# A hybrid block on one core: one of three large products goes back to eight projections, laid between the heads of linear attention, and three engines get a written order there

## The chip, the cores and the metric

The kernel runs on one core of a Trainium2 chip. A core has a matrix engine (PE, with a separate record for its weight loads, PEld), a vector engine (DVE), a scalar engine (ACT), a general engine (POOL) and a queue engine (SP) that here only starts transfers. Each executes its own list of instructions in order, and they wait for each other through semaphores. The metric is the device time of one execution in microseconds; smaller is better.

## The reference

One layer on 512 tokens of width 1024, in fp32. A normalised input is multiplied by w_in into eleven parts; two branches follow, each with a gate from the same projection, and then a feed-forward layer with a squared ReLU.

```
proj = rmsnorm(h, g_mix) @ w_in
(gq, gk, gv, gr, z_gf, z_gb, cq, ckv, kr, z_ma, z_mb) = split(proj)
y_gla = rmsnorm(o_forward + o_backward, g_gla) * silu(gr)      # linear attention, 4 heads, 256 values each
y_mla = softmax attention, 8 heads, q from rmsnorm(cq) @ w_uq, k and v from rmsnorm(ckv) @ w_ukv
merged = sigmoid(z_ma) * y_gla + sigmoid(z_mb) * y_mla
h = h + merged @ w_out;  h = h + relu(rmsnorm(h) @ w_ff1)^2 @ w_ff2;  out = rmsnorm(h, g_final)
```

The linear attention keeps a decay per key feature and token, from a log-sigmoid of a small gate (z_gf forward, z_gb backward). In the kernel z_ma is za and z_mb is zb, each 1024 features wide. The sigmoid is taken as half of 1 + tanh of half the argument.

## The kernel before

Every fp32 product is made of three passes of rounded halves (mm3, lines 88 to 90): high by high, high by low, low by high. Each operand is therefore split once: ACT copies the high half (L93) and DVE subtracts to get the low half (L94); with a scale the two are L97 and L98. Wherever a new weight is used, both engines have to pass it before PE can.

**Projections by features** (proj_begin, proj_run, proj_T). A block of 128 columns of w_in, 512 KB, is loaded on SP's queue into one of three staging buffers, split into one of four pairs of buffers, and multiplied with the eight parts of the transposed input xT: 24 matmuls of 128 features by 512 tokens. The result has features in the rows. The scale of each token, R, is multiplied in afterwards. gq and gk of each head, the eight zb blocks, ckv (two) and cq (three) are made so.

**Products of seven** (class Seven). gr, za and gv, each 1024 wide, are made with tokens in the rows by a 2 x 2 block scheme with seven block products in place of eight, in the order 1, 2, 5, 6, 3, 7, 4. Each product is 24 matmuls of 128 by 512. prepare(m) takes differences of the loaded blocks on DVE (less, L575) and splits them, two products ahead; product(m) runs the matmuls, and its ends copy (ACT, L622) or add (DVE, L627) the partial sums. A sink takes each finished piece: gr_rows (tanh, times), za_rows (tanh with half the row factor, and a multiplication into g1, which holds the gated gr), gv_rows (the split v). Between some products stands a filler: a projection that gives the other engines time (zb4, zb5, z_chunk, gq1, gk1).

**Heads of linear attention.** For each of four heads: gate_parts makes the gates (two matmuls, abs on ACT, min on DVE, exp and log, with a table load before the log and one behind it), then decays (four scans for each direction, a difference, two exps, small factors v3 and e3 on POOL and ACT). gla_qk multiplies q and k with them (four on DVE, L455, and eight products on POOL, L463). gla_scores makes the backward scores bd of four diagonal blocks, which ACT copies out (bds, L498), and then for each of four key blocks three matmuls into sc, a predicated copy of bds on DVE (L512), and a split of sc. bd and sc share four PSUM banks ("at"). gla_out multiplies the scores with v (48 matmuls), squares the result on ACT, multiplies it into g1 on DVE, and POOL makes the factor of each row. gla_turn, which comes after the scores of the next head, scales g1 by this factor, transposes it on PE (eight transposes, L688) and applies the gain on ACT.

**What sets the order.** The program is traced in Python and a planner then orders each engine's instructions by priority, costs and readiness, with tile buffers of fixed number (29 "u2", 26 "u4", four banks each of "mm" and "at"). The programmer can bind instructions of one engine to the traced order (in_program_order) or one group behind another (goes_behind). Before the change PE is bound from the products of seven to the gla_out of head 2; POOL is bound up to the end of the products; ACT and DVE are left to the planner in the heads. Gates of head h + 1 are traced ahead of the scores of head h. The last head mixes with the latent projections (ckv, cq), the rotary tables of head 1 and the first parts of softmax attention.

Of the kernel before, what the change touches and what calls it, by code (L numbers as in the profile page):

```python
# [18 lines left out]
P = 128  # L19
S = 512  # L20
NT = S // P
# [35 lines left out]
def tile_block(ctx: ExitStack, tc: tile.TileContext, t, out: bass.AP):  # L57
# [346 lines left out]
    def gate_parts(h, tag="at"):  # L404
        l = u4("l", F32)
        ms = []
        for i, d in enumerate(("f", "b")):
            bcol = (V_BF if d == "f" else V_BB) + h
            bias = gvec[:, bcol : bcol + 1]
            acc = ps(tag, f"gate{d}")  # L410
# [6 lines left out]
        nc.scalar.activation(l, l, AF.Ln, bias=1.0)  # L417
        return {d: decays(d, l[:, i], ms[i]) for i, d in enumerate(("f", "b"))}
# [220 lines left out]
    def za_rows(i, half, src, dst):  # L639
        nc.scalar.activation(dst, src, AF.Tanh, scale=r_half[:, i : i + 1])  # L640
        g = g1[i, half]
        nc.vector.scalar_tensor_tensor(g, dst, 1.0, g, op0=ALU.add, op1=ALU.mult)

# [4 lines left out]
    def mla_g2(f):  # L648

        return gated(proj_T(C_ZB + f * P, f"zb{f}"), f"b{f}")[1]  # L650

    out_rs = {}

    def gla_out(h, sc):
# [3 lines left out]
        c = slice(at, at + GDV)  # L658
        for i in range(NT):
            o = accs[i // 2][:, (i % 2) * GDV : (i % 2 + 1) * GDV]  # L660
            tok = slice(i * P, (i + 1) * P)
            for j in range(NT):
                mm3(o, sc[j][:, 0, tok], sc[j][:, 1, tok], v[j, half][:, 0, c], v[j, half][:, 1, c],
                    j == 0, j == NT - 1)
        tot = sm(f"gla{h}ss")
        for i in range(NT):
            o = accs[i // 2][:, (i % 2) * GDV : (i % 2 + 1) * GDV]
            junk = u2(f"gla{h}sq")
            nc.scalar.activation(junk[:, 0:GDV], o, AF.Square, accum_out=tot[:, i : i + 1])
            g = g1[i, half][:, c]  # L670
            nc.vector.tensor_tensor(g, o, g, op=ALU.mult)
# [3 lines left out]
        out_rs[h] = tot  # L675

    def gla_turn(h, early=None):

        half, at = h // 2, (h % 2) * GDV
        for i in range(NT):  # L680
            g = g1[i, half][:, at : at + GDV]
            nc.vector.tensor_scalar(g, g, out_rs[h][:, i : i + 1], None, op0=ALU.mult)
        began = traced()
        for dv in range(2):
# [6 lines left out]
            y = u2(f"y1{f}")  # L691
            nc.scalar.activation(y, tp, AF.Copy, scale=gla_gain[:, f : f + 1])
# [5 lines left out]
    def latent(col, n, gcol, name):  # L698
        cs, sqs = [], []
        for j in range(n):  # L700
            if j == 0:
                begun = proj_begin(w_in, col, f"{name}0")
                acc = proj_run(begun, xT)
                yield
            else:
                acc = proj_T(col + j * P, f"{name}{j}")
            c = u2(f"{name}c{j}")
            nc.scalar.activation(c, acc, AF.Copy, scale=gvec[:, gcol + j : gcol + j + 1])
            s = u2(f"{name}s{j}")
            nc.scalar.activation(s, acc, AF.Square)  # L710
            if sqs:
                nc.vector.tensor_tensor(s, s, sqs[-1], op=ALU.add)
            cs.append(c)
            sqs.append(s)
        yield
        diag = feature_rstd(sqs[-1], n * P, name, True)
        yield
        rs = spread(diag, name, "mm")
        res = []
        for j in range(n):  # L720
            nc.vector.tensor_tensor(cs[j], cs[j], rs, op=ALU.mult)
            hl = u4(f"{name}hl{j}")
            split(hl[:, 0, :], hl[:, 1, :], cs[j])
            res.append(hl)
        yield res
# [190 lines left out]
    steps = [(a, m) for a in range(3) for m in SEVEN]  # L916
# [3 lines left out]
    for n, (a, m) in enumerate(steps):  # L920
        ahead = steps[n + 2] if n + 2 < len(steps) else None
        filled = (a, m) in fillers
        if a + 1 < 3:
            for x in {3: (0,), 7: (2, 1), 4: (3,)}.get(m, ()):
                sevens[a + 1].load(x)
# [5 lines left out]
        if ahead:  # L931
            sevens[ahead[0]].prepare(ahead[1])
            if n == 2:
                more_x_sums()
        if (a, m) == (1, 5):
# [3 lines left out]
        if (a, m) == (1, 4):  # L939
            split_gates()  # L940
        if not filled:
            sevens[a].product(m)
        if a == 2 and m == 5:
            parts = gate_parts(0, "mm")
    in_program_order(summed, (mybir.EngineType.Pool,))
    near, nxt, far = gla_qk(0, parts)
    for h in range(GH):
        last = h == GH - 1
        if not last:
            parts = gate_parts(h + 1, "mm")  # L950
        began = traced()
        if last:
            next(ckv_steps)
            marks = [traced()]
            next(cq_steps)
            marks.append(traced())
            next(ckv_steps)
            marks.append(traced())
            next(cq_steps)
            goes_behind((marks[1], marks[2]), (marks[0], marks[1]), PE_ONLY)  # L960
            goes_behind((marks[2], traced()), (marks[1], marks[2]), PE_ONLY)
            ckv = next(ckv_steps)
            next(cq_steps)
            zb = proj_T(C_ZB + 6 * P, "zb6")
        projected = traced()
# [403 lines left out]
```

## Time and profile before

| | us |
|---|---|
| median of three runs | 805.8 |
| lowest, highest | 804.67, 806.24 |
| the profiled execution | 805.88 |
| its span | 803.9 |
| PE busy in the span | 766.5 |
| DVE, ACT, POOL busy | 595.8, 451.6, 103.9 |

The span runs from the first to the last instruction of the program; the profiled execution's own time is 2.0 us more. Times in rows of the profile are from the start of the span. A matmul's end is modelled and covers part of the next one, so the pace of PE is read from starts, not from the 0.39 us that one matmul of 512 columns is given. In a row of groups the columns are: how many, busy time and mean duration in ns, and the idle time of that engine before them with what ended it. In rows of stretches each engine has its busy time and number of instructions, followed by the granted clock of PE, the share of the transfer engines and their rate.

### The profile page before, as it was taken

The numbers are of one execution on the slowest core, as the hardware profiler recorded it, in microseconds if no ns is written. First come the engines' busy times: TensorE is split into PE (matmuls) and PEld (weight loads), VectorE is DVE, ScalarE is ACT, GpSimd is POOL, SyncE is SP. The second block draws the span as 40 slices with busy tenths as digits, with TensorE's granted clock in tenths as the row PEclk, the third lists the DMA queues.
The fourth block names the chain that finished last, engine by engine and source line by source line (L and its number), as shares of the span: only waits on it lengthen the run. The fifth ranks groups of instructions, "written<-read, shape, count | busy, mean of one in ns | idle before, by whom it ended". The sixth has DMA issues, their size and how long they took to land.

```text
span 803.9 us, 10168 instructions
## 1 busy us (share of the span) xinstructions
PE 766.5 (95%) x3744; PEld 645.5 (80%) x3744; DVE 595.8 (74%) x886; ACT 451.6 (56%) x761; POOL 103.9 (13%) x182
## 2 busy tenths in 40 slices
PE   9999999977868699999999999999999999999996
PEld 7778888866757688888898898888888888888885
DVE  7699787977667535889994378784878576857695
ACT  8556555665365434598882256643663366345644
POOL 0400000023523410332120100000000000000014
PEclk9999999988989799999999999999999999999999
DMA  9626243004111021323104462156014611460002
GB/s 333 204 78 187 63 114 117 0 5 124 30 27 31 23 29 50 78 62 98 53 27 163 140 221 59 48 157 183 27 53 147 177 44 53 132 183 26 27 1 104
DMA packets 87041, 73.94 MB, mean 92 GB/s; under 512 B 15088, under 2 KB 66288, under 8 KB 86992
## 3 DMA queue, kind: packets, MB, share of 16 engines
q1 hardware_dynamic: 85904, 70.14, 29.3%
q10 hardware_dynamic: 864, 2.38, 0.8%
q0 software_dynamic: 224, 0.79, 0.3%
q8 instruction: 29, 0.48, 0.3%
q14 instruction: 20, 0.16, 0.1%
HBM read 69.62 MB, written 2.10 MB: 89 GB/s over the span
## 4 chain that ended last, share of the span: by engine, by line
PE 80%; DVE 8%; ACT 5%; issue 2%; DMA 2%; POOL 2%; SPq 1%; POOLq 0%; ACTq 0%; DVEq 0%
PE f L89 7%; PE f L90 7%; PE f L88 7%; PE gx L88 4%; PE gx L89 4%; PE gx L90 4%; PE wo L90 2%; PE wo L89 2%; PE gz L89 2%; PE gz L90 2%; PE gz L88 2%; PE wo L88 2%; PE tp L877 1%; DMA grw<-in_w_in 1%; DVE gvw L575 1%
## 5 line engine op out<-in xcount | busy, mean ns | idle before, releaser
L1133 DVE TENSOR_TENSOR w<-w,w 128x1024 f32<-128x1024 f32 x32 | 38.7, 1221 | 0.4
L1308 POOL DMA_DIRECT2D gfin<-in_g_final x1 | 0.7, 653 | 282.7 <-PE f L90 282.7
L506 PE MATMUL sc<-qkf 128*128 128x128 f32 x32 | 7.9, 335 | 17.5 <-ACT bds L498 17.5
L863 ACT ACTIVATE e<-s,top 128x512 f32<-128x512 f32 x32 | 22.1, 694 | 2.6 <-DVE top L860 2.4
L1080 DVE TENSOR_TENSOR h<-gx,h 128x512 f32<-128x512 f32 x32 | 21.6, 685 | 1.8 <-PE gx L90 1.8
L94 DVE TENSOR_TENSOR pT<-tp,pT 128x512 fp32r<-128x512 f32 x32 | 21.7, 680 | 1.0 <-ACT pT L93 0.7
L506 PEld LDWEIGHTS sc<-qkf 128*128 128x128 f32 x32 | 6.7, 232 | 19.3 <-ACT bds L498 18.7
L860 DVE TENSOR_REDUCE top<-s 128x1 f32<-128x512 f32 x32 | 21.8, 681 | 0.1
L93 ACT ACTIVATE pT<-tp 128x512 fp32r<-128x512 f32 x32 | 19.2, 600 | 3.4 <-PE tp L877 3.3
L877 PE MATMUL tp<-ident,e 128*128 128x128 f32 x128 | 19.3, 273 | 0.2
L88 PE MATMUL av<-pT,v 128*128 128x256 f32 x64 | 19.1, 298 | 0.0
L1186 ACT ACTIVATE fa<-f 128x512 f32<-128x512 f32 x32 | 18.5, 578 | 0.0
L877 PEld LDWEIGHTS tp<-ident,e 128*128 128x128 f32 x128 | 15.2, 140 | 4.1 <-ACT e L863 0.7
L89 PE MATMUL av<-pT,v 128*128 128x256 f32 x64 | 18.4, 287 | 0.0
L90 PE MATMUL av<-pT,v 128*128 128x256 f32 x64 | 18.2, 284 | 0.0
L93 ACT ACTIVATE gbh<-y 128x512 fp32r<-128x512 f32 x16 | 10.2, 635 | 14.0 <-DVE y L1203 14.0
L895 POOL TENSOR_TENSOR tb<-tb,y 128x512 f32<-128x512 f32 x8 | 11.2, 1400 | 50.3 <-DVE tb L894 36.0
L93 ACT ACTIVATE b_20h<-w 128x1024 fp32r<-128x1024 f32 x7 | 7.4, 1059 | 12.1 <-PE gz L90 6.0
L93 ACT ACTIVATE b_10h<-w 128x1024 fp32r<-128x1024 f32 x7 | 7.4, 1059 | 12.1 <-PE gz L90 6.0
L93 ACT ACTIVATE b_00h<-w 128x1024 fp32r<-128x1024 f32 x7 | 7.4, 1057 | 12.0 <-PE gz L90 6.0
L88 PE MATMUL s<-kbuf,q 96*128 96x512 f32 x32 | 13.9, 436 | 0.2 <-DVE pT L94 0.2
L1195 ACT ACTIVATE px<-fa 128x256 f32<-128x256 f32 x32 | 13.4, 419 | 1.0
(1638 smaller groups left out, 2912.9 us busy)
## 6 DMA issues: line engine op xcount, KB each, us to landing
w<-in_w_ff SPq DMA_DIRECT2D x64, 256.0 KB, 3.6
grw<-in_w_in SPq DMA_DIRECT2D x8, 512.0 KB, 7.8
zaw<-in_w_in SPq DMA_DIRECT2D x8, 512.0 KB, 4.2
gvw<-in_w_in SPq DMA_DIRECT2D x8, 512.0 KB, 4.9
x<-in_xt SPq DMA_DIRECT2D x8, 256.0 KB, 5.1
vw<-in_w_first SPq DMA_DIRECT2D x8, 256.0 KB, 5.2
h<-in_x ACTq DMA_DIRECT2D x4, 512.0 KB, 5.1
out<-ms SPq DMA_DIRECT2D x7, 256.0 KB, 2.2
```

The lines of the kernel that those rows point to most:

```text
L88: nc.tensor.matmul(acc, lh, rh, start=start, stop=False, skip_group_check=onto)
L89: nc.tensor.matmul(acc, lh, rl, start=False, stop=False, skip_group_check=onto)
L90: nc.tensor.matmul(acc, ll, rh, start=False, stop=stop, skip_group_check=onto)
L93: nc.scalar.activation(hi, src, AF.Copy)
L94: rest.tensor_tensor(lo, src, raw(hi), op=ALU.subtract)
L506: nc.tensor.matmul(sc[:, dj], near["f"][:, 1, j], near["f"][:, 0, j], start=True, stop=True)
L860: nc.vector.tensor_reduce(top, acc, axis=AX.X, op=ALU.max, negate=True)
L863: nc.scalar.activation(e, acc, AF.Exp, bias=top, accum_out=tot)
L877: nc.tensor.transpose(tp[:, k * P : (k + 1) * P], e[:, k * P : (k + 1) * P], ident)
L1080: nc.vector.tensor_tensor(hc, acc, hc, op=ALU.add)
L1133: nc.vector.tensor_tensor(wq[dst][g], wq[x][g], wq[y][g], op=op)
L1186: nc.scalar.activation(a, acc, AF.Relu)
```

## The change

za is no longer a product of seven. It becomes eight projections by features, za0 to za7, two for each head of linear attention. za_gate multiplies the result by R, takes the tanh and turns it into gain x (1 + tanh) with one ACT operation; gla_turn multiplies this with the transposed output on DVE, in place of the gain on ACT. gla_out is split in three: the matmuls (gla_out), the squares and the row factor (gla_squares), and one DVE operation that applies row factor and gate together (gla_gated) in place of two.

gate_parts is split into gates_begin (up to the log) and gates_end (the decays). The generator for the latent projections becomes a class with the same steps. In the seven scheme gv now follows gr; z_chunk moves to gr's product 7, gq1 to gv's product 2, and the loads and splits of the gates move with them. gv's last two products, gk1 and zb5 are written out ahead of the heads.

In the heads the scores come first, then the next head's gates. From the first gate to the turn of head 2, ACT and DVE (SPLITTERS) are bound to the traced order and PE's bound order is extended to the same point. The rotary tables are traced after this stretch. The turn of each of the first three heads now comes at the end of its own head.

```diff
+    def za_gate(f, acc):
+
+        z = u2(f"za{f}")
+        nc.vector.tensor_tensor(z, acc, R, op=ALU.mult)
+        nc.scalar.activation(z, z, AF.Tanh, scale=0.5)
+        gain = gla_gain[:, f : f + 1]
+        nc.scalar.activation(z, z, AF.Identity, bias=gain, scale=gain)
+        za_gates[f] = z
...
+    def gla_gated(h, os, rs):
+
+        half, at = h // 2, (h % 2) * GDV
+        for i, o in enumerate(os):
+            g = g1[i, half][:, at : at + GDV]
+            nc.vector.scalar_tensor_tensor(g, o, rs[:, i : i + 1], g, op0=ALU.mult, op1=ALU.mult)
...
-            y = u2(f"y1{f}")
-            nc.scalar.activation(y, tp, AF.Copy, scale=gla_gain[:, f : f + 1])
+            y = za_gates.pop(f)
+            nc.vector.tensor_tensor(y, tp, y, op=ALU.mult)
...
-    sevens = [Seven(C_GR, "gr", gr_rows), Seven(C_ZA, "za", za_rows), Seven(C_GV, "gv", gv_rows)]
+    sevens = [Seven(C_GR, "gr", gr_rows), Seven(C_GV, "gv", gv_rows)]
...
-        (0, 2): lambda: zb_gate(4), (0, 7): lambda: zb_gate(5), (1, 2): lambda: z_chunk("mm"),
-        (1, 7): lambda: project_qk(1, 0), (2, 7): lambda: project_qk(1, 1),
+        (0, 2): lambda: zb_gate(4), (0, 7): lambda: z_chunk("mm"),
+        (1, 2): lambda: project_qk(1, 0),
...
+    heads_from = traced()
+    gated_now = gates_begin(0)
+    w_k = begin_qk(1, 1)
+    parts = gates_end(gated_now)
+    sevens[1].product(7)
     near, nxt, far = gla_qk(0, parts)
+    w_b = begin(C_ZB + 5 * P, "zb5")
+    qk[1, 1] = qk_normed(1, 1, proj_run(w_k, xT))
+    sevens[1].product(4)
+    w_a = begin_za(0)
+    g2.append(gated(proj_run(w_b, xT), "b5")[1])
+    ckv_, cq_ = Latent(C_CKV, 2, V_KV, "ckv"), Latent(C_CQ, 3, V_Q, "cq")
+    for h in range(GH - 1):
         sc = gla_scores(near, nxt, far)
+        gated_now = gates_begin(h + 1)
+        w_b = begin_za(2 * h + 1)
+        acc = proj_run(w_a, xT)
+        parts = gates_end(gated_now)
+        za_gate(2 * h, acc)
+        os = gla_out(h, sc)
+        near, nxt, far = gla_qk(h + 1, parts)
+        if h < 2:
+            w_a = begin_qk(h + 2, 0)
         else:
+            ckv_.begin(0)
+        rs = gla_squares(h, os)
+        za_gate(2 * h + 1, proj_run(w_b, xT))
+        if h < 2:
+            w_b = begin_qk(h + 2, 1)
+            gla_gated(h, os, rs)
+            qk[h + 2, 0] = qk_normed(h + 2, 0, proj_run(w_a, xT))
+            w_a = begin_za(2 * h + 2)
+            qk[h + 2, 1] = qk_normed(h + 2, 1, proj_run(w_b, xT))
+        else:
+            ckv_.run(0)
+            ckv_.begin(1)
+            gla_gated(h, os, rs)
+            ckv_.run(1)
+            cq_.begin(0)
+        gla_turn(h)
+    in_program_order(heads_from, SPLITTERS)
+    in_program_order(ordered, PE_ONLY)
...
+    h = GH - 1
+    cos, sin = rotary_tables()
...
+    sc = gla_scores(near, nxt, far)
...
+    za_gate(6, proj_T(C_ZA + 6 * P, "za6"))
...
+    za_gate(7, proj_T(C_ZA + 7 * P, "za7"))
```

More of the change, by code (lines that the diff above doesn't have):

```diff
@@ L919, in tile_block @@
         sevens[a].prepare(m)
-    for n, (a, m) in enumerate(steps):
-        ahead = steps[n + 2] if n + 2 < len(steps) else None
+    for n, (a, m) in enumerate(steps[:-2]):
+        ahead = steps[n + 2]
         filled = (a, m) in fillers
-        if a + 1 < 3:
+        if a == 0:
             for x in {3: (0,), 7: (2, 1), 4: (3,)}.get(m, ()):
-                sevens[a + 1].load(x)
+                sevens[1].load(x)
         if filled:
@@ L930, in tile_block @@
             goes_behind((at, traced()), loading, (mybir.EngineType.SP,))
[L931 to L935, printed above, removed]
+        sevens[ahead[0]].prepare(ahead[1])
+        if n == 2:
+            more_x_sums()
+        if (a, m) == (0, 5):
             load_gates()
@@ L1000, in tile_block @@
+    kbuf = rotary_k()
+    zb = proj_begin(w_in, C_ZB + 7 * P, "zb7")
+    at = traced()
+    proj_run(zb, xT, None, range(3))
+    mid = traced()
+    ro = rotary_q()
+    goes_behind((mid, traced()), (at, mid), PE_ONLY)
+    g2.append(gated(proj_run(zb, xT, None, range(3, KD)), "b7")[1])
+    for _ in up_units(0):
+        pass
+    os = gla_out(h, sc)
+    rs = gla_squares(h, os)
+    gla_gated(h, os, rs)
     LAG_B, LAG_C = 3, 6
```

169 lines of the change are left out of this document (70 added, 99 removed).

## The prediction

> **What bounds the kernel now.** I read the page first (span, granted clock), then the table of busy time by stretches with its edges laid on the stages, then the waits, and last the timeline of one head, engine by engine.
>
> ```profile
> span 803.9 us, 10168 instructions
> ...
> PEclk9999999988989799999999999999999999999999
> ...
> 40.60:92.15 51.55, 49.60 (x218) 40.39 (x216) 47.11 (x56) 29.02 (x38) 1.94 (x4) 1.00 0.42 128
> 92.15:139.30 47.15, 47.15 (x210) 39.04 (x209) 39.46 (x45) 26.37 (x35) 0.00 (x0) 1.00 0.33 98
> 139.30:167.10 27.80, 27.80 (x123) 22.71 (x121) 26.59 (x35) 20.47 (x26) 3.35 (x6) 1.00 0.00 0
> 167.10:195.30 28.20, 19.71 (x75) 15.72 (x74) 18.95 (x23) 16.18 (x22) 5.02 (x15) 0.86 0.28 75
> 195.30:224.00 28.70, 26.16 (x130) 22.85 (x131) 19.73 (x36) 11.23 (x24) 16.18 (x33) 0.84 0.14 37
> 224.00:255.40 31.40, 24.50 (x139) 21.71 (x138) 23.59 (x42) 18.49 (x33) 10.80 (x26) 0.89 0.13 34
> 255.40:288.35 32.95, 24.67 (x137) 21.80 (x136) 18.50 (x39) 18.06 (x33) 11.26 (x27) 0.84 0.12 23
> 288.35:340.20 51.85, 51.85 (x287) 44.74 (x286) 33.14 (x61) 24.87 (x49) 9.98 (x12) 1.00 0.26 50
> ```
>
> Columns: stretch, its length, then busy time and count for PE, PEld, DVE, ACT, POOL, then the clock. The stretches are gr (40.6), za (92.15), gv (139.3), the end of gv (167.1), heads 0, 1 and 2 of linear attention, and the last head up to attention. PE is full everywhere except in the four rows from 167.1 to 288.35. There it sits idle for 8.5, 2.5, 6.9 and 8.3 us, and the clock column is below 1. Nothing else in front of PE is worth moving; the question is what those four rows hold.
>
> ```profile
> PE sc L506 <- ACT bds L498: 17.5, 3, 8.3
> ...
> 224.51 0.67 ACT L412 ACTIVATE l<-gatef,gvec 128x512 f32<-128x512 f32 x1
> 225.08 0.68 ACT L412 ACTIVATE l<-gateb,gvec 128x512 f32<-128x512 f32 x1
> 225.79 1.06 ACT L416 ACTIVATE l<-l 128x1024 f32<-128x1024 f32 x1
> 226.87 1.28 ACT L417 ACT_TABLE_LOAD   x1
> 228.16 1.06 ACT L417 ACTIVATE l<-l 128x1024 f32<-128x1024 f32 x1
> 229.23 1.28 ACT L441 ACT_TABLE_LOAD   x1
> ...
> 233.98 0.58 ACT L498 ACTIVATE bds<-bd 128x512 f32<-128x512 f32 x1
> 234.46 0.62 ACT L434 ACTIVATE eeb<-difb 128x512 f32<-128x512 f32 x1
> ...
> 224.03 1.05 PE L494 MATMUL bd<-qkb 128*128 128x128 f32 x8
> 224.92 0.39 PE L506 MATMUL sc<-qkf 128*128 128x128 f32 x2
> ...
> 225.80 0.39 PE L506 MATMUL sc<-qkf 128*128 128x128 f32 x2
> ...
> 234.62 0.80 PE L506 MATMUL sc<-qkf 128*128 128x128 f32 x2 [6.90 <-ACT bds L498]
> ...
> 243.73 0.28 PE L88 MATMUL gla1o<-gv,sc 128*128 128x256 f32 x1
> ...
> 249.49 0.40 PE L88 MATMUL gk<-xT,gk3h 128*128 128x512 f32 x1
> ```
>
> The waits and head 1 tell why. The scores write bd and four sc tiles into four banks, so the fourth sc needs bd's bank, which the 0.58 us copy bds frees. That copy stands on ACT behind the gates of the next head (abs, exp, two table loads, log): bd is done by 225, bds runs at 233.98. PE waits 6.90 us for half a microsecond of work.
>
> **What PE needs and what it loses.** In the za row PE is never idle: seven products of 24 matmuls, one more projection of 24 (gq1) and z_chunk's 16 make 208 in 47.15 us, 0.2267 each, so 24 cost 5.44 and a pair of gates 0.45. From the starts above: bd 0.89, a score block 0.88, so scores 4.41; gla_out 249.49 - 243.73 = 5.76; the eight transposes of a turn, like bd's eight, 0.89. The four low rows hold 9 x 24 matmuls (gv7, gk1, gv4, gq2, gk2, gq3, gk3, ckv0, ckv1), three scores, three gla_out, three gate pairs, two turns: 49.0 + 13.2 + 17.3 + 1.35 + 1.8 = 82.6 us of work in 121.25. **38.6 us** are lost there, 26 idle and the rest to half clock. That is all the change can win back.
>
> **PE work of the change.** za loses 7 x 24 matmuls and gains 8 x 24: **+5.44**. All other products are the same and only move (zb5, gk1, gv7 and gv4 into the fixed sequence, z_chunk into gr, gq1 into gv, the third turn ahead of the last head, za6 and za7 into the last head).
>
> **What it loses afterwards** needs the new order laid out by hand with these rows.
>
> ```profile
> L93 ACT ACTIVATE sc<-sc 128x512 fp32r<-128x512 f32 x12 | 6.5, 595 | 0.0
> L93 ACT ACTIVATE ckv0h<-ckv0f 128x1024 fp32r<-128x1024 f32 x1 | 1.1, 1063 | 4.9 <-PE gq L89 4.9
> L708 ACT ACTIVATE ckvc<-ckv,gvec 128x512 f32<-128x512 f32 x1 | 0.7, 682 | 0.0
> ...
> L94 DVE TENSOR_TENSOR sc<-sc,sc 128x512 fp32r<-128x512 f32 x12 | 7.6, 685 | 3.0 <-ACT sc L93 3.0
> L426 DVE TENSOR_TENSOR_SCAN rrf<-mf,l 128x128 f32<-128x128 f32 x12 | 5.3, 500 | 3.4 <-ACT l L417 3.4
> L426 DVE TENSOR_TENSOR_SCAN rrb<-mb,l 128x128 f32<-128x128 f32 x12 | 4.3, 402 | 0.0
> L455 DVE TENSOR_TENSOR qkb<-gkn,eeb 128x512 f32<-128x512 f32 x3 | 3.3, 1100 | 0.0
> L512 DVE COPY_PREDICATED sc<-after,bds 128x128 f32<-128x128 int32 x12 | 3.0, 296 | 5.5 <-ACT bds L498 4.1 <-PE sc L508 1.4
> L455 DVE TENSOR_TENSOR qkb<-gqn,eeb 128x512 f32<-128x512 f32 x3 | 2.0, 682 | 0.0
> L94 DVE TENSOR_TENSOR ckv0l<-ckv0f,ckv0h 128x1024 fp32r<-128x1024 f32 x1 | 1.7, 1664 | 0.2 <-ACT ckv0h L93 0.2
> L94 DVE TENSOR_TENSOR ckv1l<-ckv1f,ckv1h 128x1024 fp32r<-128x1024 f32 x1 | 1.2, 1226 | 0.2 <-ACT ckv1h L93 0.2
> ```
>
> Neighbours on an engine overlap by about 0.1 us (225.08 starts before 224.51 + 0.67), so I lay them 0.1 closer than they last; a scan steps 0.32.
>
> Head h, time 0 at bd. The scores now stand ahead of the gates on ACT, so bds ends at 1.7 (behind the last multiplication of the turn before, at 1.1) and the fourth sc, at 3.5, waits for nothing: **the 17.5 us are gone**. What is late next? In the fixed order DVE and ACT hand each score tile to and fro (predicated copy, high half, low half: 1.6), the next beginning after: 8.4 for four. ACT is free at 7.75: two abs 9.1, exp 10.15, table 11.45, log 12.5, high half of za's second weights 13.55; DVE its low half 14.8, four scans and a difference 16.75, again for the other direction 18.7; ACT two exps and e3 20.15, tanh and Identity of the first za gate (priced like sc's copies) 21.4, high half of gq's weights 22.45. DVE meanwhile z (19.4) and the four products of gla_qk (22.8; two at 0.68, two at 1.1 beside POOL), then gq's low half, 1.23 alone or 1.66 beside POOL: 24.1 to 24.5. PE reaches gq at 4.41 + 0.45 + 5.44 + 5.76 + 5.44 = 21.5, runs the two matmuls that need no low half, and waits: 24.3 - 21.95 = **2.4 us**, in each of heads 0, 1 and 2 (ckv0 there). The first za projection and gla_out (sc ready at 8.4, wanted at 10.3) and the second za (14.8, wanted at 16.1) wait for nothing, gk's low half (28.7) is ahead of PE's 29.7. The gating by row factor is now one DVE operation for two, with POOL's factor due by 33 and some 4 us early.
>
> Head 2 has two more: ckv1's split begins only after ckv0's two copies: 0.68 + 0.6 + 1.06 + 1.23 less overlaps and the two early matmuls = **3.0**; cq0's the same behind ckv1, less the turn's 0.89: **2.2**.
>
> Before head 0 (zero at the end of gv's product 3): gates first, ACT two sinks, abs, exp, table, log, gk1's high half 7.5, low half 8.8; PE, done with product 7 at 5.9, waits 2.4. Product 4 adds onto the banks that DVE must first have read for product 7, and these reads stand behind all scans: scans and differences from 8.8 to 12.8, first read 13.5, ACT's high half of v behind the last exp 14.9, DVE's low half 15.6 (each near 0.7, like sc's), second read 16.3. PE wants that bank at 8.8 + 22 x 0.2267 + 0.7 = 14.5: 1.8. Then gla_qk ends at 21.1 and zb5's low half, behind it, at 22.4; PE has finished product 4 at 21.1 and two matmuls at 21.5: 0.9. Together 5.1, with rounding **5.2**.
>
> So the waits are 5.2 + 3 x 2.4 + 3.0 + 2.2 = 17.6.
>
> **Clock.** What a gap costs beside itself:
>
> ```profile
> 54.38 0.50 PE L90 MATMUL zb<-xT,zb4l 128*128 128x512 f32 x1 [1.63 <-DVE zb4l L94]
> ...
> 204.35 0.79 PE L506 MATMUL sc<-qkf 128*128 128x128 f32 x2 [2.29 <-ACT bds L498]
> ...
> 204.35:212.35 8.00, 8.00 (x30) 6.70 (x31) 6.58 (x12) 3.06 (x7) 2.61 (x5) 0.79 0.01 2
> ```
>
> After 1.63 us the clock stays at 1.00 (the gr row). After 2.29 us, 6.32 us of work (one score block, 24 matmuls) took 8.00: 1.7 lost. My six longer gaps (gk1, three heads, ckv1, cq0) lie around 2.29, most with two matmuls inside. Ends: 0 and 6 x 1.7 = 10.2. I take two, **3.4**: the 3.0 gap and one of the rest. Here the Trainium skill, "TensorE: Matmul & The Clock Gate", section "HAM oscillation", differs: only gaps beyond about 3.4 us throttle. By that rule this term is 0 and the time 791; the 2.29 us row speaks against it.
>
> **Smaller edits.**
>
> ```profile
> zaw<-in_w_in SPq DMA_DIRECT2D x8, 512.0 KB, 4.2
> ```
>
> The rotary tables are traced behind the loop and can slip into head 2's ACT queue: between 0 and two table loads (2 x 1.28) with two activations (1.2), 3.8; I take **1.0**, since DVE has holes there. gr and gv: z_chunk instead of zb5 and the gate splits raise DVE's load in stages that are 91 to 96% full (47.11 of 51.55, 26.59 of 27.80); cost 0, hidden by PE's own products, at worst once more the 1.63 us. Weight loads: as many bytes for za, eight 512 KB transfers on SP's queue in either form; with three staging buffers each is issued some 20 us ahead of a landing that took 4.2. z_chunk, the gate loads and the positions are issued one stage earlier, on SP's and POOL's queues; zb5's load stood where z_chunk's two stand now, POOL is busy 1.94 us in that whole stage, and nothing waits for the gates' small transfers before the heads: 0, and a late z_chunk would cost PE its lateness, up to another 1.6 us as above. za6 and za7 lie in a row where PE is full and DVE busy 33 of 52 us: they cost their matmuls, no more.
>
> **Sum.** 5.44 - 38.6 + 17.6 + 3.4 + 1.0 = -11.2. The profiled execution took 805.88 (span 803.9 and 2.0 around it), the median is 805.8: **794.6 us**.
>
> **Rivals.**
> A: the handing over is tighter than I laid it, or ACT's sinks come in a better order; waits of 9 or 10 us and a warm clock. 5.4 - 38.6 + 9.5 = -23.7: 782. For it: PE has 49 us of filler there. Against: the chain of 24 us is made of measured rows.
> B: each head's chain comes 3 us later (a small operation ahead in one of the queues that can no longer be passed, an e3 that waits for POOL): 3 x 3 more, 803.6. For it: nothing in a fixed queue overtakes; every delay before gq's low half reaches PE in full.
> C, slower: DVE beside POOL becomes the bound. Scans average 0.50 in the f row against 0.40 in the b row, products 1.10 against 0.68, a low half 1.66 against 1.23. If POOL's products of one head ran beside the scores and scans of the next, the chain would grow by 4 x 0.4 + 8 x 0.35 + 2 x 0.4 + 4 x 0.4 + 2 x 0.43 = 7.7 us a head: 3 x 7.7 plus three more cold starts, 5.1: 823. It decides from 3.7 us a head on. Against it: POOL is busy 16 of 28.7 us in head 0 and is fed by gla_qk in the second half of a head, so it should be quiet by the next scores. The Trainium skill, "SBUF — State Buffer", section "SBUF: two separate sides", calls the port of DVE and GpSimd an exclusive lock that blocks the loser fully; these rows show a slowdown of 0.4 us, not a whole POOL operation.
>
> **Chances.** Forecast (787 to 801) 0.55, A 0.15, B 0.18, C 0.12. From about 780 to 806 hold all but C and a little. No change here means within 0.2% (1.6 us), about what this measurement can tell: faster 0.55 + 0.15 + 0.13, same 0.04, slower 0.13. The likeliest alone lies between 787 and 801.
>
> **What would show it.** The fourth sc without a wait for bds; a wait of some 2.4 us before gq2, gq3 and ckv0, ended by the low half of their weights on DVE; ckv1 about 3; some 5 between gv's last products and zb5; head 0 and 1 near 36 us each (33.3 of work). Wrong it would be if a head lasted over 40, if a wait for a buffer or for POOL's row factor turned up on DVE, or if the stretch from attention on (340.2 before) changed in length.

## The result and the profile after

The changed kernel takes 792.85 us (median of four runs, 792.16 to 795.3). The kernel before, run beside it, takes 805.23 (804.66 to 806.24). The ratio is 0.985 with a 95% interval of 0.9826 to 0.9875, so the change is faster by 12.4 us, or 1.5%. The forecast was 794.6, most likely between 787 and 801, in a range of 780 to 806.

The profiled execution took 793.04, against 805.88 before; its span is 12.6 us shorter. First the page's line of the span and the table by stretches, with the columns of the prediction's table (length, busy time and count of PE, PEld, DVE, ACT and POOL, then the clock, the share of the transfer engines and their rate). The edges lie on the stages of the new order: gr (40.62), gv (91.27), the stretch ahead of head 0 (125.22), heads 0, 1 and 2 (153.41, 188.35, 223.35), the last head (265.90) and attention to the end (327.07).

```profile
span 791.3 us, 10153 instructions
...
40.62:91.27 50.65, 48.07 (x209) 38.80 (x208) 46.12 (x57) 29.97 (x41) 1.81 (x3) 1.00 0.37 106
91.27:125.22 33.95, 32.98 (x146) 26.95 (x144) 28.48 (x30) 16.80 (x21) 0.00 (x0) 1.00 0.13 32
125.22:153.41 28.19, 23.41 (x100) 18.09 (x99) 20.86 (x31) 16.18 (x22) 11.41 (x24) 1.00 0.16 41
153.41:188.35 34.94, 33.84 (x187) 29.01 (x186) 21.07 (x38) 19.89 (x34) 13.27 (x27) 1.00 0.22 59
188.35:223.35 35.00, 33.91 (x189) 29.03 (x187) 21.70 (x40) 19.38 (x33) 13.32 (x27) 1.00 0.23 61
223.35:265.90 42.55, 36.87 (x191) 30.19 (x189) 22.15 (x42) 23.03 (x39) 12.23 (x25) 0.96 0.19 49
265.90:327.07 61.17, 61.17 (x323) 52.79 (x324) 42.95 (x73) 33.27 (x61) 12.96 (x17) 1.00 0.44 97
327.07:791.30 464.23, 456.41 (x2267) 384.48 (x2265) 340.42 (x510) 256.87 (x457) 31.64 (x37) 1.00 0.30 93
```

Before, four rows stood at a clock of 0.84 to 0.89 with 26 us of idle PE. After, only head 2 is below 1.00 (0.96). Idle PE is now 4.8 us ahead of head 0, 1.1 in each of heads 0 and 1, and 5.7 in head 2. Two stages that were nearly full have larger holes: gr 2.6 where it had 1.95, and gv 1.0 where it had none. The last stretch keeps its length.

Then the list of PE's waits (total, times, longest).

```profile
PE ckv L88 <- ACT ckv1h L93: 2.2, 1, 2.2
PE gk L88 <- ACT gk1h L93: 2.1, 1, 2.1
...
PE gvx L88 <- DVE gvc L632: 1.4, 1, 1.4
PE cq L88 <- ACT cq0h L93: 1.3, 1, 1.3
PE gq L90 <- DVE gq1l L94: 1.0, 1, 1.0
...
PE zb L90 <- DVE zb5l L94: 0.8, 1, 0.8
PE grz L88 <- ACT grc L627: 0.7, 1, 0.7
```

The line that led this list before, the scores waiting 17.5 us for bds, is gone. What stands there now are mostly splits of weights: PE arrives at a projection and the high half (ACT, L93) or the low half (DVE, L94) isn't there yet. The rows of gvx and grz are waits for a bank, which a sum on DVE (gvc) or a copy on ACT (grc) has to free. The timeline of head 0 shows how close it is. PE's rows come first, then DVE's of the same moment.

```profile
175.67 0.50 PE L88 MATMUL gq<-xT,gq2h 128*128 128x512 f32 x1 [0.57 <-ACT gq2h L93]
...
176.93 0.50 PE L90 MATMUL gq<-xT,gq2l 128*128 128x512 f32 x1 [0.53 <-DVE gq2l L94]
```

```profile
174.34 0.68 DVE L460 TENSOR_TENSOR qkb<-gkn,eeb 128x512 f32<-128x512 f32 x1
175.65 1.23 DVE L94 TENSOR_TENSOR gq2l<-gq2f,gq2h 128x1024 fp32r<-128x1024 f32 x1 [0.64 <-ACT gq2h L93]
```

gq2's split is traced behind gla_qk, and in a bound queue it stays there. Its low half ends at 176.88, which is 23.5 us after the head's start at 153.41; PE was there at 175.1. The forecast had laid it at 24.3. Now the same point in head 2, ACT's rows and then PE's.

```profile
252.18 0.69 ACT L720 ACTIVATE ckvc<-ckv,gvec 128x512 f32<-128x512 f32 x1 [3.25 <-PE ckv L90]
252.76 0.59 ACT L722 ACTIVATE ckvs<-ckv 128x512 f32<-128x512 f32 x1
253.24 1.05 ACT L93 ACTIVATE ckv1h<-ckv1f 128x1024 fp32r<-128x1024 f32 x1
```

```profile
254.35 0.50 PE L88 MATMUL ckv<-xT,ckv1h 128*128 128x512 f32 x1 [2.21 <-ACT ckv1h L93]
...
255.61 0.79 PE L90 MATMUL ckv<-xT,ckv1l 128*128 128x512 f32 x1 [0.53 <-DVE ckv1l L94]
...
264.64 0.50 PE L88 MATMUL cq<-xT,cq0h 128*128 128x512 f32 x1 [1.34 <-ACT cq0h L93]
...
265.90 0.50 PE L90 MATMUL cq<-xT,cq0l 128*128 128x512 f32 x1 [0.52 <-DVE cq0l L94]
```

ACT is idle for 3.25 us until ckv0's matmuls are done, then copies ckv0 twice, and only then turns to ckv1's weights, which don't depend on ckv0 at all. The order as written makes PE wait for ACT and ACT for PE.

### The profile page after: what moved, and what is told of

The parts are those of the page before. It is cut to its first block, busy times and chain, and to the rows that moved or that the text cites. A ratio compares the mean times of both kernels' runs of the same rounds, so it can differ in the third digit from the quotient of the medians.

```text
span 791.3 us, 10153 instructions
## 1 busy us (share of the span) xinstructions
PE 765.2 (97%) x3768; PEld 641.6 (81%) x3768; DVE 572.5 (72%) x858; ACT 442.7 (56%) x749; POOL 107.5 (14%) x182
## 4 chain that ended last, share of the span: by engine, by line
PE 79%; DVE 11%; ACT 8%; issue 2%; POOL 1%; DMA 0%; SPq 0%; POOLq 0%; DVEq 0%; ACTq 0%
PE f L89 7%; PE f L90 7%; PE f L88 7%; PE gx L88 4%; PE gx L89 4%; PE gx L90 4%; PE first L311 2%; PE wo L88 2%; PE wo L89 2%; PE gz L89 2%; PE wo L90 2%; PE gz L90 2%; PE gz L88 2%; PE tp L891 2%; PE zb L90 1%
## 5 line engine op out<-in xcount | busy, mean ns | idle before, releaser
L94 DVE TENSOR_TENSOR pT<-tp,pT 128x512 fp32r<-128x512 f32 x32 | 21.6, 678 | 0.8 <-ACT pT L93 0.7
L442 POOL COPY v3f<-rrf 128x4 f32<-128x4 f32 x4 | 2.8, 709 | 138.2 <-DVE rrf L431 138.2
L93 ACT ACTIVATE pT<-tp 128x512 fp32r<-128x512 f32 x32 | 19.0, 595 | 4.0 <-PE tp L891 3.8
L909 POOL TENSOR_TENSOR tb<-tb,za 128x512 f32<-128x512 f32 x8 | 11.2, 1402 | 54.8 <-DVE tb L908 40.4
L93 ACT ACTIVATE gbh<-y 128x512 fp32r<-128x512 f32 x16 | 10.1, 634 | 14.0 <-DVE y L1257 14.0
L94 DVE TENSOR_TENSOR sc<-sc,sc 128x512 fp32r<-128x512 f32 x16 | 10.9, 690 | 9.5 <-ACT sc L93 9.5
L93 ACT ACTIVATE sc<-sc 128x512 fp32r<-128x512 f32 x16 | 9.3, 596 | 11.5 <-DVE sc L517 11.5
L93 ACT ACTIVATE b_10h<-w 128x1024 fp32r<-128x1024 f32 x7 | 7.4, 1059 | 12.1 <-PE gx L90 6.0
L93 ACT ACTIVATE b_20h<-w 128x1024 fp32r<-128x1024 f32 x7 | 7.4, 1059 | 12.1 <-PE gx L90 6.0
L93 ACT ACTIVATE b_00h<-w 128x1024 fp32r<-128x1024 f32 x7 | 7.4, 1057 | 12.0 <-PE gx L90 6.0
```

The costliest lines, as they stand in the source:

```text
L93: nc.scalar.activation(hi, src, AF.Copy)
L94: rest.tensor_tensor(lo, src, raw(hi), op=ALU.subtract)
```

## Experiments

All of this left two questions. Where does the gain come from, and what do the waits that remain cost? Two theories stood against each other for the first. **Order**: the gain comes from putting the scores ahead of the next head's gates; the projections of za are only work moved. **Filler**: the gain comes from the six projections of za in the heads, which keep PE busy while ACT and DVE run the chain of the gates. For the second, the splits that come late can be moved, or the queues can be left free.

Kernels were timed in several series, each with the kernel before beside them; its medians there were 804.0 to 805.7, so differences between two series are good to one or two us. Each ratio is to the kernel before in the same series.

### The old layout with the scores ahead of the gates

```diff
     for h in range(GH):
         last = h == GH - 1
-        if not last:
-            parts = gate_parts(h + 1, "mm")
         began = traced()
...
         goes_behind((projected, scored), (began, projected), PE_ONLY)
+        if not last:
+            parts = gate_parts(h + 1, "mm")
         if h:
             gla_turn(h - 1, (projected, scored))
```

> The kernel before with one edit: the gates of head h + 1 are traced behind the scores of head h, so that ACT meets bds first. za stays a product of seven, no order of ACT and DVE is written out. Theory 'order' (what was lost in the heads was bds standing behind the next gates on ACT): the 17.5 us wait goes, with some 6 us of half clock; PE has 22.4 us of work in a head, and the new chain (scores, gates 10.4, four products 3.3) is about 20 to 24, so heads last 23 to 26 in place of 28.7, 31.4 and 33.0: 783 to 792 us, at least as good as the change itself, without its 24 extra matmuls. Theory 'filler' (PE had nothing to run there, and the eight za projections are what fills the holes): the wait only moves from the fourth sc to the next bd and stays 5 to 7 us a head: 800 to 806.

Measured: 796.61 us, ratio 0.9896 (0.9876 to 0.9916). That is neither what the order theory said nor what the filler theory said. Its list of PE's waits tells what happened.

```profile
PE bd L494 <- DVE qkb L455: 4.8, 1, 4.8
PE gq L88 <- DVE mf L414: 4.4, 1, 4.4
PE gvx L88 <- ACT gvb L622: 4.1, 1, 4.1
...
PE sc L506 <- ACT bds L498: 0.3, 1, 0.3
```

The wait for bds falls from 17.5 to 0.3 us. But two others (4.8 and 4.1) stand ahead of head 0, where this edit touches nothing (they were 4.3 and 4.1 before), and in the heads a new one takes over: gq3 waits 4.4 us for a bank that holds a gate until DVE has read it (mf). DVE's timeline shows why that read is late.

```profile
224.19 0.95 DVE L682 TENSOR_SCALAR gra<-gra,gla0ss 128x256 f32<-128x256 f32 x2 [4.05 <-POOL gla0ss L674]
...
231.63 0.74 DVE L414 TENSOR_SCALAR mf<-gatef,gvec 128x512 f32<-128x512 f32 x1
```

DVE waits 4.05 us for POOL's row factor, has splits of the scores in between, and reads the gate only at 231.63. The scores are early now, and the gates pay for it: without more PE work in the head, PE arrives before them.

### The change without the bound order of ACT and DVE

```diff
         gla_turn(h)
-    in_program_order(heads_from, SPLITTERS)
     in_program_order(ordered, PE_ONLY)
```

> The changed kernel without the written order of ACT and DVE in the heads; PE's order stays. Theory 'late splits' (what PE still waits for in the heads are splits of weights that the written order puts behind the decays or behind the copies of the product before): the planner may split as soon as a buffer is free, a head ahead; the waits before gq2, gq3 and ckv0 (1.7 each), ckv1 (3.2 and 1.7 of clock) and cq0 (2.2) go, some 12 us, of which a few come back elsewhere: 781 to 787. Theory 'the written order earns its keep': the planner lets splits and copies stand ahead of bds and the gates again, and it is slower than the change by 3 us or more: 796 to 806.

Measured: 776.29 us, ratio 0.9648 (0.9632 to 0.9664). It is below both ranges. The lower one counted only waits in the heads; ahead of head 0 another 5.8 us go. The stretch ahead of head 0, and head 1:

```profile
125.39:147.80 22.41, 22.41 (x99) 18.31 (x98) 20.14 (x31) 17.64 (x24) 9.52 (x22) 1.00 0.26 72
...
182.58:215.88 33.30, 33.30 (x189) 29.18 (x188) 22.27 (x40) 19.38 (x34) 11.90 (x27) 1.00 0.28 76
```

The 28.19 us ahead of head 0 become 22.41 without a hole, and head 1 is as long as its work. The planner takes splits early, as one row of DVE shows.

```profile
149.25 1.63 DVE L94 TENSOR_TENSOR gq2l<-gq2f,gq2h 128x1024 fp32r<-128x1024 f32 x1
```

That is 1.5 us after the start of head 0 at 147.80 and some 20 us before PE wants it (171.28); bound to the traced order it began 22.2 us after the start (175.65 - 153.41). So the written sequence of ACT and DVE costs 16.6 us of what the rest of the change brings.

### The splits that come late, one by one

Three runs keep the bound order and move only the place where splits are written. First the latent projections of head 2 (run and begin exchanged, begun kept per index).

```diff
         else:
-            ckv_.run(0)
             ckv_.begin(1)
+            ckv_.run(0)
+            cq_.begin(0)
             gla_gated(h, os, rs)
             ckv_.run(1)
-            cq_.begin(0)
         gla_turn(h)
```

> The changed kernel with two lines swapped twice in head 2: the split of ckv1's weights is written ahead of ckv0's run, that of cq0's ahead of ckv1's run. Theory 'late splits': the waits before ckv1 (2.4 and 0.7), its half clock (1.7) and the waits before cq0 (1.5 and 0.7) go: 6 to 7 us less, about 786. Rival: PE would only wait for the next thing there (row factor, gating), and under 2 us are won: 791 to 793.

Measured: 785.53 us, ratio 0.9763 (0.9747 to 0.9779), 7.3 less than the change. This is what the waits for ckv1 and cq0 and the half clock behind ckv1 were worth.

Then gq's split (ckv0's in head 2) ahead of the decays.

```diff
         acc = proj_run(w_a, xT)
+        if h < 2:
+            w_a = begin_qk(h + 2, 0)
+        else:
+            ckv_.begin(0)
         parts = gates_end(gated_now)
         za_gate(2 * h, acc)
         os = gla_out(h, sc)
         near, nxt, far = gla_qk(h + 1, parts)
-        if h < 2:
-            w_a = begin_qk(h + 2, 0)
-        else:
-            ckv_.begin(0)
         rs = gla_squares(h, os)
```

> The changed kernel with the split of gq's weights (ckv0's in head 2) written ahead of the decays in place of behind gla_qk. Theory 'late splits': the three waits of 1.7 go, and the decays, 1.2 us later, are not missed because the next bd has them some 12 us ahead: 5 us less, about 788. Rival 'the vector chain of a head is the bound': what is put ahead of the decays delays za's gates and the turn by as much, and the time stays at 792 to 794.

Measured: 789.13 us, ratio 0.9808 (0.9789 to 0.9828), 3.7 less. The three waits are gone from its trace, but head 2 now has two pieces with a mean clock of 0.75 in place of one (251.10 to 258.00, and 261.47 to 268.36, shown under the hardware, below), which takes some of it back.

> The changed kernel with its written order, but with the splits of gq (ckv0), ckv1 and cq0 ahead: both earlier edits at once. Theory 'late splits': the two gains add, 7.3 and 3.7, as they are waits at different places: 781 to 783. What is left against the planner's order (776.3) is then the stretch ahead of head 0, 6.0 us of waits. Rival 'a bound queue costs by itself': one of the gains is swallowed by another wait in the same head: 785 or more.

Both edits together: 781.48 us, ratio 0.97 (0.9686 to 0.9715). The gains add: 7.3 + 3.7 = 11.0, measured 11.4. What is left against the free queues is the stretch ahead of head 0. There the last edit begins the bound order at head 0.

```diff
-    heads_from = traced()
     gated_now = gates_begin(0)
...
+    heads_from = traced()
     for h in range(GH - 1):
         sc = gla_scores(near, nxt, far)
```

> As the run with all splits ahead, but the written order of ACT and DVE begins only at head 0; the stretch from the first gates to zb5 is left to the planner. Theory 'late splits': the 6.0 us of that stretch go, and with the splits in time a written order costs nothing against the planner's: 776 to 777.5. Rival 'a bound queue costs by itself': 2 us or more stay against the planner's 776.3: 778.5 or more.

Measured: 775.56 us, ratio 0.9625 (0.9611 to 0.964), 5.9 less than with both edits alone and the lowest time of all that compute the whole layer (0.7 below the free queues, which is within what two series can tell). So in the heads a bound order as such costs nothing. The 17.3 us between the change and this kernel are 11.4 for splits written too late in the heads and 5.9 ahead of head 0. There two splits came late and the read of a bank stood behind the scans; whether that stretch can be bound without loss wasn't tried.

### za as a product of seven in the new order

With free queues (776.29) two runs put za back as a product of seven between gr and gv. The new heads, without their projections of za, stay otherwise as they are.

```diff
-    sevens = [Seven(C_GR, "gr", gr_rows), Seven(C_GV, "gv", gv_rows)]
+    sevens = [Seven(C_GR, "gr", gr_rows), Seven(C_ZA, "za", za_rows), Seven(C_GV, "gv", gv_rows)]
...
-        (0, 2): lambda: zb_gate(4), (0, 7): lambda: z_chunk("mm"),
-        (1, 2): lambda: project_qk(1, 0),
+        (0, 2): lambda: zb_gate(4), (1, 2): lambda: z_chunk("mm"),
+        (1, 7): lambda: project_qk(1, 0),
...
-        w_b = begin_za(2 * h + 1)
-        acc = proj_run(w_a, xT)
+        if h < 2:
+            project_qk(h + 2, 0)
...
-        za_gate(2 * h + 1, proj_run(w_b, xT))
```

> The run with the planner's order of ACT and DVE, but with za again as a product of seven between gr and gv, and no projections of za in the heads; gates behind scores, the new sequence ahead of head 0, PE's order and everything else stay. PE has 24 matmuls less (5.44 us) and 22.4 us of work in a head in place of 33.3. In the run with the planner's order the products that the next bd needs are ready 23.7 us after this head's bd, POOL's some 3 us later. Theory 'filler': PE waits 1 to 4 us in each of three heads, some at half clock, and the 5.44 us are given back: 775 to 781. Theory 'order is all': the chain shortens with the work that is gone from ACT and DVE, nothing waits, and it is 5 us faster than with the projections: 770 to 772.

Measured: 796.13 us, ratio 0.9879 (0.9862 to 0.9895): worse than either theory said. The turn stands at the end of its own head, and without the two projections of za PE reaches its transposes too soon. The waits of PE, and DVE's row behind the longest of them:

```profile
PE y L704 <- DVE gra L694: 11.1, 2, 5.8
PE y L704 <- DVE grb L694: 4.6, 1, 4.6
```

```profile
212.46 0.88 DVE L694 SCALAR_TENSOR_TENSOR gra<-gla0o,gla0ss,gra 128x256 f32<-128x256 f32 x2 [4.48 <-POOL gla0ss L686]
```

This run was unfair to the seven: it showed that the turn cannot stay there without filler, not what za as a product of seven could do. So the next one moved the turn behind the scores of the next head, where it stood in the kernel before.

```diff
         gated_now = gates_begin(h + 1)
+        if h:
+            gla_turn(h - 1)
...
             cq_.begin(0)
-        gla_turn(h)
```

> The run with za as a product of seven in the new order waited 5.8, 5.4 and 4.6 us at the transposes of the turn, for the gating of its own head. Here the turn stands behind the scores of the next head, as before the change; nothing else differs. Theory 'filler': the vector work between one bd and the next (about 24 us, POOL's products up to 27) is longer than PE's 22.4 us of a head, so the wait moves to bd, sc or the next product and stays 2 to 5 us a head with some half clock: 778 to 790. Theory 'the turn stood in the wrong place': without that wait nothing is missing, and it comes out below the projections by their 5.4 us: 770 to 773.

Measured: 786.92 us, ratio 0.9771 (0.9756 to 0.9785). It has 5.4 us less PE work than 776.29 and takes 10.6 more. PE's waits:

```profile
PE sc L511 <- DVE gra L694: 3.3, 1, 3.3
PE gq L88 <- DVE mf L415: 3.3, 1, 3.3
PE ckv L88 <- DVE mf L415: 2.8, 1, 2.8
```

The same waits as in the first experiment (the row factor, the bank with the gate). Between the second and the third, from 220.27 to 247.37, the mean clock is 0.94. The filler theory holds, for this placing. Whether a third placing of the turn, or a row factor on another engine than POOL, would let the seven run without waits wasn't tried.

### One projection of za less

From the free version (776.29), one of the eight projections of za is taken out, with its weights. The gate of za6 serves twice, so this kernel leaves out a part of the layer.

```diff
-    za_gate(7, proj_T(C_ZA + 7 * P, "za7"))
+    za_gates[7] = u2("za7")
+    nc.vector.tensor_copy(za_gates[7], za_gates[6])
```

> The run with the planner's order without za7: its weights, split, 24 matmuls and gate are left out, and the gate of za6 is used for both (one copy on DVE). If PE is the bound to the end, a projection costs its 24 matmuls: 5.4 us less, 770.9. If the last head has slack on PE's side or another engine sets its end there, under 2 us are won: 774 to 776.

Measured: 770.88 us, ratio 0.9569 (0.9555 to 0.9584), 5.4 less than 776.29 (of another series; 775.56, the kernel of its own series with all matmuls, is 4.7 above it). Within what series can tell, one projection more or less is worth its 24 matmuls (5.44) once PE has no holes: PE is then the bound.

### The gates ahead of the scores again

Two runs undo the order in the free version (776.29), za staying as projections. The first moves the gates up to the log ahead of the scores.

```diff
-        sc = gla_scores(near, nxt, far)
         gated_now = gates_begin(h + 1)
+        sc = gla_scores(near, nxt, far)
```

> The run with the planner's order of ACT and DVE, za by projections, and one thing undone: the gates of head h + 1 are traced ahead of the scores of head h again. Theory 'order': ACT meets abs, exp, log and the tables before bds again, the fourth sc waits 5 to 8 us in three heads with half clock behind it, and the projections, which stand behind the scores on PE, can't fill that: 793 to 802. Theory 'filler': the projections leave PE work enough, the wait is shorter than 2 us a head: 776 to 783.

Measured: 778.14 us, ratio 0.9663 (0.9646 to 0.968). This looks like a blow to the order theory, but it undid only half: the decays still stood behind the scores, and the planner let bds pass ahead of the log in head 0 (bds at 153.93, the table load at 154.52), and one wait of 2.1 us for it came back, not three. It tells little. The second moves gates and decays.

```diff
-        sc = gla_scores(near, nxt, far)
-        gated_now = gates_begin(h + 1)
+        parts = gates_end(gates_begin(h + 1))
+        sc = gla_scores(near, nxt, far)
...
-        parts = gates_end(gated_now)
```

> The run with gates first left the decays behind the scores, and the planner let bds pass right behind the exp. Here gates and decays of head h + 1 are both traced ahead of the scores of head h, which is the order of the kernel before; za stays by projections, ACT and DVE by the planner. Theory 'order': the copy bds stands behind the whole chain again, the fourth sc waits 6 to 9 us in each of three heads with 2 to 3 us of half clock behind, as it did before the change: 796 to 806, all of the gain against the kernel before gone but the stretch ahead of head 0 (11.4 us there before). Theory 'filler': with 33 us of PE work a head the wait shrinks to 2 us or less: 777 to 783.

Measured: 804.87 us (ten runs, 803.98 to 806.13), ratio 1.001 (1.0 to 1.0021). The whole gain is gone, with the six projections still in the heads. PE's wait, and ACT's rows in head 0:

```profile
PE sc L511 <- ACT bds L503: 22.5, 3, 9.7
```

```profile
154.06 1.28 ACT L418 ACT_TABLE_LOAD   x1
...
156.43 1.28 ACT L446 ACT_TABLE_LOAD   x1
...
161.44 0.58 ACT L503 ACTIVATE bds<-bd 128x512 f32<-128x512 f32 x1
```

It is the picture of the kernel before: bds behind two table loads and behind the first exps of the decays, as there. So both theories were half right:

| | za as product of seven | za as projections |
|---|---|---|
| gates and decays ahead of the scores | 805.23 (the kernel before) | 804.87 |
| scores ahead of the gates | 796.61 (old layout), 786.92 (new) | 776.29 |

The four cells differ in more than their row and column. All but the kernel before and 796.61 have the new sequence ahead of head 0 as well, and it has a price of its own. The start of head 0 divides the two; these are its rows in the kernel before, in 786.92 and in 804.87 (in 776.29 it is at 147.80).

```profile
195.31 0.58 PE L494 MATMUL bd<-qkb 128*128 128x128 f32 x1 [4.35 <-DVE qkb L455]
```

```profile
184.27 1.05 PE L499 MATMUL bd<-qkb 128*128 128x128 f32 x8
```

```profile
148.49 1.05 PE L499 MATMUL bd<-qkb 128*128 128x128 f32 x8
```

za as projections takes 7 x 5.44 = 38.08 us of matmuls away ahead of this point and puts 8 x 5.44 = 43.52 behind it. A pair of gates (0.45) lies ahead of it in the first and third of these kernels and behind it in the others. With za's matmuls taken out, the spans of the profiled executions differ from the kernel before (803.9) by:

| run (differences in us) | ahead of head 0 | from head 0 on | the extra projection | span |
|---|---|---|---|---|
| order, old layout (796.61) | +0.4 | -9.3 | 0 | -8.9 |
| order, new layout (786.92) | -11.0 | -8.5 | 0 | -19.5 |
| projections without the order (804.87) | -8.7 | +2.5 | +5.4 | -0.8 |
| both, free queues (776.29) | -9.4 | -25.0 | +5.4 | -29.0 |
| the change (792.85) | -3.8 | -14.2 | +5.4 | -12.6 |

From head 0 on, the order alone brings some 9 us in either layout, the projections alone cost 2.5 besides their matmuls, and both together bring 25.0. The projections cover the chain that the order leaves behind, and only where that order is there to be covered. The 9 to 11 us ahead of head 0 are a third part that neither theory had: they come with the new sequence of gv's last products, gk1 and zb5, in every run that has it, and the change itself lost more than half of them to its bound order. Which step of that sequence brings them wasn't tried.

## Why the prediction was right

The mechanism came as described. The size is in part luck: terms that were too high by 4.8 us together (the waits in the heads, the clock, the rotary tables) stood against terms that were too low by 3.1 (gr and gv, the stretch ahead of head 0, ckv1).

**The 17.5 us for bds: right.** Gone in the list of waits. That the place of the gates causes them is shown by the run with gates and decays ahead, where 22.5 come back.

**PE work, +5.44: right.** Leaving out one projection gave 5.4.

**Waits in the heads, 3 x 2.4: too high.** A head has 33.27 us of work by the prediction's rows (4.41 + 0.45 + 4 x 5.44 + 5.76 + 0.89); heads 0 and 1 took 34.94 and 35.00, so 1.7 each is lost, of it 1.1 as idle time in front of the two halves and the rest in matmuls next to a gap, which start 0.34 apart in place of 0.23. The place (gq's low half behind gla_qk) was right. What was too long in my chain is the work beside POOL: two products of gla_qk were laid at 1.1 and took 0.68, as in the row above, and the low half took 1.23. Only 0.8 us of that reached PE (23.5 for 24.3), since DVE then waited 0.64 for the high half on ACT.

**ckv1 3.0, cq0 2.2: right.** Idle 2.21 + 0.53 and 1.34 + 0.52; with the matmuls around them 3.2 and 2.2.

**Ahead of head 0, 5.2: a little low.** The three waits are there, for the reasons given: 2.10 + 0.53 for gk1 (2.4 was laid), 1.36 for gv's bank (1.8), 0.79 for zb5 (0.9), together 4.8. But the stretch lost 6.0 (28.19 less 4 x 5.44 and a pair of gates, 0.45), since four gaps each cost a little beside their idle time.

**Clock, two cold starts of 1.7: one.** Only the gap ahead of ckv1 was followed by half clock. The longest gap was the one named first.

**gr and gv, 0: wrong by 2.1.** This is the term that failed in kind: I held DVE's and ACT's extra load there to be hidden by PE's own products. gr has 8 matmuls less than before (1.8 us) and is only 0.9 shorter; gv has gq1 more (5.44) and a pair of gates less (0.45) and is 6.15 longer, 1.2 too much. In gv it fits the load: with the gates' splits among its rows (92.91 and 94.88), DVE works without a gap until gq1's low half ends at 103.69, and PE waits 0.97 for it. In gr the load is not the cause. DVE's rows there start within 0.1 us of where they started before, but the planner put ACT's copy grc behind the last piece of xsz instead of ahead of it. First the row before, then those after.

```profile
67.64 1.06 ACT L622 ACTIVATE grc<-grz 128x512 f32<-128x512 f32 x2
```

```profile
70.03 0.63 ACT L93 ACTIVATE xsz<-xz 128x512 fp32r<-128x512 f32 x1 [2.33 <-DVE xz L557]
70.56 1.07 ACT L627 ACTIVATE grc<-grz 128x512 f32<-128x512 f32 x2
```

ACT now stands idle for 2.33 us ahead of that piece, the copy comes 2.9 us later, and PE waits 0.69 for the bank at product 3. Neither wait was in the prediction, and the bound that it gave, 1.63, was too low for both together. The 1.63 for zb4 was there before too.

**Rotary tables, 1.0: 0.** They ran in DVE's holes around the turn of head 2, and PE did not wait for them.

With what was measured the sum is 5.44 - 38.6 + 6.0 + 3 x 1.7 + 3.2 + 2.2 + 1.7 + 2.1 = -12.9. The span fell by 12.6. The rest of 0.3 is within what the tail after attention differs by (464.23 against 463.7 before).

**The rivals.** A (782) and B (803.6) were sizes of the same chain; it came out between A and the forecast, nearer to the latter. C (823, DVE beside POOL) did not happen, and the rows that would have shown it are in the groups of DVE in the heads:

```profile
L431 DVE TENSOR_TENSOR_SCAN rrf<-mf,l 128x128 f32<-128x128 f32 x12 | 4.1, 404 | 0.0
L431 DVE TENSOR_TENSOR_SCAN rrb<-mb,l 128x128 f32<-128x128 f32 x12 | 4.1, 403 | 0.0
```

The scans of the f row took 500 ns on average before; now both rows stand at 403 or 404, so POOL is quiet beside them. A wait for POOL's row factor did turn up on DVE, which the prediction had named as a sign of trouble:

```profile
183.50 0.88 DVE L689 SCALAR_TENSOR_TENSOR gra<-gla0o,gla0ss,gra 128x256 f32<-128x256 f32 x2 [2.21 <-POOL gla0ss L681]
```

It cost PE nothing here: PE had gk2's matmuls to run until the turn at 187.48. In the runs without projections of za in the heads, where PE reaches that point sooner, it was 4.05 to 4.49 us long and ended in a wait of PE each time.

**What the prediction did not see** is not in its sum. It took the written order as given and priced its waits. Nearly all of them came from the place at which a split (ahead of head 0 also the read of a bank) is written in a bound queue, and not from a lack of time on ACT or DVE: 775.56 has the same operations and takes 17.3 us less.

## What to carry to other kernels

When a small copy that frees a bank stands behind a long chain in an in-order queue, move the copy ahead first, but ask what the chain itself then makes late: from head 0 on it was worth some 9 us alone, and 25 once 10.9 us of independent matmuls a head covered what was left. Binding the queues to a written order cost nothing in the heads where every split of weights was written a step ahead of its use, and 11 us where some were written only where first needed. Price an extra product by its matmuls against the idle time it fills: eight projections for a product of seven cost 5.4 us and saved some 16. And where two theories of a gain are tested against each other, compare the runs stage by stage: here 9 us lay in a stretch that neither theory was about.

## What the runs showed of the hardware

The clock does not follow the length of a gap alone. The gap ahead of gk1 is the same in the change and in the kernel with all splits ahead: 2.10 us, two matmuls, then 0.53 or 0.52. The two windows that follow hold the rest of gk1's matmuls, first of the change (with the piece behind ckv1 below it), then of the other kernel.

```profile
134.63:139.90 5.27, 5.27 (x23) 4.40 (x24) 4.49 (x11) 2.53 (x7) 2.97 (x12) 1.00 0.37 99
255.61:262.27 6.66, 6.66 (x22) 5.29 (x23) 2.33 (x6) 0.00 (x0) 0.00 (x0) 0.76 0.31 79
```

```profile
134.44:141.34 6.90, 6.90 (x23) 5.53 (x24) 5.50 (x13) 3.12 (x7) 3.52 (x16) 0.75 0.28 77
```

A clock of 1.00 with 5.27 us in one, 0.75 with 6.90 in the other, from a gap of the same length that began 0.2 us earlier. The kernel with only the latent splits moved, an edit in head 2, has the same gap too, and 6.86 us at 0.75 behind it. And the shortest gap with half clock behind it was ahead of cq0 in the run with gq's split early: 1.33 us, two matmuls, 0.52, and then this row.

```profile
261.47:268.36 6.89, 6.89 (x25) 5.54 (x25) 6.69 (x9) 1.84 (x3) 0.00 (x0) 0.75 0.68 177
```

The same gap in the change (1.34 and 0.52) had none. So gaps of about 1.9 to 2.7 us in two pieces cost 0 or about 1.7 us more, and here the trace of one kernel doesn't tell which it will be in the next. The Trainium skill, "TensorE: Matmul & The Clock Gate", section "HAM oscillation", warns only of gaps beyond about 3.4 us; these rows disagree. The Trainium skill, "TensorE: Matmul & The Clock Gate", Part 1, section "What's actually happening", says that the activity window runs freely and does not start with the kernel. What is seen here, the same gap with and without half clock at slightly different times, agrees with that; no run here shows the window itself.
